# Splitting three weight blocks ahead instead of two, and moving the row flips, in the paired experts of a mixture of 32

## The chip, the cores and the metric

The kernel runs on one core of one Trainium2 chip. The metric is the device time of one execution in microseconds (us); the number that counts is the median of several runs. All engines of the core take part: TensorE (PE), VectorE (DVE), ScalarE (ACT), GpSimd (POOL) and SyncE (SP), whose queue issues the weight transfers.

## The reference, cut to what matters

Two transformer blocks work on 512 rows of 1024 numbers in float32. The second one holds a mixture of 32 experts, four of which are chosen for each row. Only the time of this mixture is touched by the change:

```python
def moe(x, w_router, b_router, w_up, b_up, w_down, b_down):
    ...
    top_v, top_i = lax.top_k(logits, TOP_K)
    w = jax.nn.softmax(top_v, axis=-1)
    flat_e = top_i.reshape(-1)
    order = jnp.argsort(flat_e)
    sorted_e = flat_e[order]
    tok = order // TOP_K
    sizes = jnp.bincount(flat_e, length=N_EXPERTS).astype(jnp.int32)
    xs = xf[tok]
    h = lax.ragged_dot(xs, w_up, sizes) + b_up[sorted_e]
    g, lin = jnp.split(h, 2, axis=-1)
    g = jnp.minimum(g, SWIGLU_LIMIT)
    lin = jnp.clip(lin, -SWIGLU_LIMIT, SWIGLU_LIMIT)
    act = g * jax.nn.sigmoid(SWIGLU_ALPHA * g) * (lin + 1.0)
    y = lax.ragged_dot(act, w_down, sizes) + b_down[sorted_e]
    y = y * w.reshape(-1)[order][:, None].astype(y.dtype)
    return jax.ops.segment_sum(y, tok, num_segments=n).reshape(B, T, D)
```

Here D is 1024 and so is the hidden width, so an expert has 1024x2048 numbers of `w_up` and 1024x1024 of `w_down`, 12.6 MB in all.

## The kernel before, in words

**Blocks and buffers.** The experts are put in an order by their number of rows. The weights of one expert are 12 blocks of 128x2048 float32 (1 MiB each), eight of `w_up2` and four of `w_dn2`, in the sequence of the table `ORDER`. Block n of the whole stream lies in raw buffer n % 8 (`raws`), and `refill(n)` puts the fetch of block n+8, into the buffer that block n leaves, on SP's queue (L1122). The eight buffers carry four names in the listings below: `b_12206` for blocks 0, 1, 8, 9 of a large expert, `pp` for 2, 3, 10, 11, `b_12225` for 4, 5 and `b_12343` for 6, 7.

**A large expert** (`expert`, up to 128 rows) computes with split weights: ACT copies a block into a rounded high part (L219), DVE subtracts it from the block for the low part (L220), and both go into one of four pairs of tiles (block n into pair n % 4). The pairs are called `wh`/`wl` (two of them), `raw` and `b_12224` here. `part` then runs 12 matmuls a block (L1322). After up blocks 3, 5 and 7 the gated product (`gated`, L1345 to L1349) is made on ACT and DVE, and after blocks 5, 8 and 9 it is transposed on PE (`flip`, L1303) and split, as the down blocks' left side `h`. Down blocks 8 and 9 need its first half, 10 and 11 the second.

**A small expert** (`few`, up to 64 rows) multiplies the raw block as it lies (`halves`, L1517 and L1521), without a split.

**The order of the run.** Here the large expert 0 comes first, then eleven pairs of a small expert and a large one (`pairs`), and nine small ones at the end. In the first four pairs the large expert has a second pass (`two`, `SECOND = 4`) with 32 more rows, which multiplies the raw blocks, so that their buffers are refilled only behind that pass.

**Work ahead.** In a paired small expert, blocks 0 and 1 of the large one are split after the small one's blocks 10 and 11 (`unfold`) and not yet refilled. In the large expert, iteration i splits block i+2, refills that buffer, and for i = 0, 1 refills the buffer of block i too. `ahead` also issues the gather of the rows of the expert after the next (POOL, L1289, at i = 2) and transposes the next expert's rows at i = 8 and 9 of a small expert (`flip`, L1303), each half being split by ACT and DVE (0.5 MB of rows for a large expert). The instructions are written in program order; a scheduler then sets each engine's own order, and that is what the listings in the section on the change show.

Below, Lk is block k of the large expert of a pair, and a pair is counted from its small expert's first matmul.

Of the kernel before, what the change touches and what calls it, by code (L numbers as in the profile page):

```python
# [25 lines left out]
NE, TT = 32, 128  # L26
# [131 lines left out]
class K:  # L158
# [941 lines left out]


    ORDER = [("w_up2", c, i) for c in range(8) for i in (c,)] + [("w_dn2", 0, 0), ("w_dn2", 1, 2), ("w_dn2", 0, 1), ("w_dn2", 1, 3)]
    RAW, PAIRS = 8, 4
    TAIL = 0, 1, 4, 3, 2

    def moe_weights(self):
# [17 lines left out]
    def raw(self, n):  # L1124
        return self.raws[n % self.RAW if n < NE * 12 else self.TAIL[n - NE * 12]]

    def unfold(self, n):
        wh, wl = self.pairs[n % self.PAIRS]
        self.split(wh, wl, self.raw(n))
        if n % 12 > 1 or n >= NE * 12:  # L1130
            self.refill(n)

    def refill(self, n):
# [8 lines left out]
    def moe(self):  # L1142
        tc, nc, a = self.tc, self.nc, self.a
        with ExitStack() as es:
            mp = es.enter_context(tc.tile_pool(name="mp", bufs=1))
            m = self.m
            m["mm"] = [self.pm(n, 512) for n in ("mm", "mm", "lg", "lg")]
            m["bb"] = [self.pm("pv", 512) for i in range(2)]
            m["tr"] = [self.pm("tr", 4, 128) for i in range(2)]
            self.ntr = 0  # L1150
            w = lambda n: self.wp.tile([128, 2048], F32R, name=n)
            b2 = self.big.tile([128, 2, 2048], F32R, name="b2")
            b3 = self.big.tile([128, 2, 2048], F32, name="b3")
            self.raws += [b3[:, i] for i in range(2)]
            self.pairs = [(w("wh"), w("wl")), (w("wh"), w("wl")), (w("raw"), w("raw")),
                          tuple(b2[:, i] for i in range(2))]
            b4 = self.big.tile([128, 4, KC, 128], F32R, name="b4")
            m["x"] = [(b4[:, 0], b4[:, 1]), (b4[:, 2], b4[:, 3])]
            self.b4 = b4
            h = mp.tile([128, 2, KC, 128], F32R, name="h")  # L1160
            m["h"] = h[:, 0], h[:, 1]
            xb = self.xb
            m["xb"] = xb[:, 0], xb[:, 1]
            b5 = self.big.tile([128, 4, D], F32, name="b5")
            m["xg"] = [mp.tile([128, D], F32, name="xg"), b5[:, 0]]
            for i, n in enumerate(("y", "act", "actb")):
                m[n] = [b5[:, 1 + i]]
            m["sg"] = mp.tile([128, 512], F32, name="sg")
            m["one"] = [mp.tile([128, 2, 128], F32R, name=f"one{i}") for i in range(2)]
            m["oh"] = [mp.tile([128, TB, 128], BF, name=f"oh{i}") for i in range(2)]  # L1170
            m["xs"] = mp.tile([128, KC, 32], F32, name="xs")
            m["xf"] = mp.tile([128, KC, 64], F32, name="xf")
            m["seven"] = mp.tile([128, 2], F32, name="seven")
            for i, v in enumerate((7.0, float(np.float32(1.702) * np.float32(7.0)))):
                nc.vector.memset(m["seven"][:, i:i + 1], v)
            self.noh = 0
            m["sl"] = [self.slot_tiles(mp, f"s{i}") for i in range(4)]
            self.identb = mp.tile([128, 128], BF, name="identb")
            nc.vector.tensor_copy(self.identb, self.ident)
            m["jb"] = mp.tile([128, 1], F32, name="jb")  # L1180
            m["pos"] = mp.tile([128, TB, 1], F32, name="farpos")
            srt = self.const(mp, "sort")
            m["far"] = mp.tile([128, 2], F32, name="far")
            m["frw"] = mp.tile([128, TB, 1, 6], BF, name="frw")
            m["fw"] = mp.tile([128, TB, 1], F32, name="fw")
            self.slots(m["sl"][0], self.posm[:, :, 0:1], self.rw[:, :, 0:1], only=3)
            nc.vector.memset(m["xg"][1], 0.0)
            first = self.gather(m["xg"][0], m["sl"][0], 0)
            with tc.issue_after(first.ins):
                for n in range(4, 6):  # L1190
                    self.fetch(n, nc.gpsimd)
            self.order(srt)
            b0 = self.big.tile([128, 2, 2048], F32, name="b0")
            self.raws += [b0[:, i] for i in range(2)]
            for n in range(6, self.RAW):
                self.fetch(n)
            for n in range(2):
                self.unfold(n)
            self.select(0)
            self.flip(m["xg"][0], m["x"][0], whole=m["xf"])  # L1200
            self.places(srt)
            for i in (2, 3):
                self.unfold(NE * 12 + i)
            self.embed(self.big.tile([128, TB, D], F32, name="b0"))
        self.rts.close()
# [145 lines left out]
    def bank(self, e, i):  # L1351

        mm, s = self.m["mm"], 2 * (e % 2)
        if i < 8:
            return mm[(s + i // 2) % 4]
        return mm[(s + i % 2) % 4]
# [59 lines left out]
    def expert(self, e, two=False):  # L1416

        nc, m = self.nc, self.m
        one, x, act = m["one"][e % 2], m["x"][e % 2], m["act"][0]
        bank = partial(self.bank, e)  # L1420
        self.numbers(e)
        if two:
            self.second_rows()
        for i in range(12):
            n = e * 12 + i
            if i < 10:
                self.split(*self.pairs[(n + 2) % self.PAIRS], self.raw(n + 2))
                if not two:
                    self.refill(n + 2)
            if i < 2 and not two:  # L1430
                self.refill(n)
            self.part(bank(i), x if i < 8 else m["h"], i, self.pairs[n % self.PAIRS], one)
            if two:
                for k in range(i + (i > 0), min(i + 2, 12)):
                    self.second(k, e)
                    self.refill(e * 12 + k)
            if i == 0 and e:
                self.finish(e - 1, False)
            self.ahead(e, i, 6, False)
            self.swiglu(i, bank, act)  # L1440
            if i in (5, 8, 9):
                self.flip(act, m["h"], *{5: (0, 4), 8: (4, 6), 9: (6, 8)}[i])
        if two:
            self.second_finish()
        self.finish(e, True)
# [77 lines left out]
    def few(self, e, paired=False, second=False):  # L1523

        nc, m = self.nc, self.m
        self.numbers(e)
        xf, act = m["xf"], m["act"][0][:, :512]
        hf = m["y"][0][:, :512].rearrange("p (t a r) -> p t a r", t=4, a=2)
        h = lambda k: hf[:, k % 2, k // 2] if k < 4 else hf[:, k % 2 + 2, k // 2 - 2]
        for i in range(12):  # L1530
            n = e * 12 + i
            self.halves(self.bank(e, i), (lambda k: xf[:, k]) if i < 8 else h, i, e)
            self.refill(n)
            if i > 9 and (paired or e == NE - 1):
                self.unfold(n + 2)
            if i == 0 and e and e % 2 == 0:
                self.finish(e - 1, False)
            self.ahead(e, i, 8, paired)
            if i == 3 and second:
                self.further(e + 1)  # L1540
            if i in (3, 5, 7):
                j = i // 2
                pg, pl = [self.bank(e, k)[:, :256] for k in (0, 2)] if j == 1 else \
                    [self.bank(e, i)[:, 128 * k:128 * k + 128] for k in range(2)]
                self.gated(pg, pl, self.side(act, j, 64))
            if i in (5, 8, 9):
                t0, t1 = {5: (0, 2), 8: (2, 3), 9: (3, 4)}[i]
                p = self.tr()
                for t in range(t0, t1):
                    nc.tensor.transpose(p[:, t - t0], act[:, 128 * t:128 * t + 128], self.ident)  # L1550
                nc.vector.tensor_copy(hf[:, t0:t1].rearrange("p t a r -> p t (a r)"), p[:, :t1 - t0])
            if e == NE - 1 and i == 6:
                self.last_rows(e)
        if e % 2 == 0:
            self.finish(e, False)
        if e == NE - 1:
            self.last(e)

    def ahead(self, e, i, at, both):

        m = self.m
        if i == 1 and e == 0 or i == 6 and e % 4 == 1 and e + 3 < NE:
            f = e // 4 * 4 + 4 if e else 0
            self.slots(m["sl"][f // 4 % 2], self.posx[:, :, f:f + 4], self.rw[:, :, f:f + 4])
        for f in [e + 2] * (i == 2) + [1] * (i == 1 and e == 0):
            if f < NE:
                self.gather(m["xg"][f % 2], m["sl"][f // 4 % 2], f % 4, 64 if f % 2 or at == 8 and e else 128)
        if i == 2 and e + 1 < NE:
            self.select(e + 1)
        if i in (at, at + 1) and e + 1 < NE:  # L1570
            f, k = (e + 1) % 2, 4 * (i - at)
# [367 lines left out]
```

## Time and profile before

| what | us |
|---|---|
| median of 3 runs | 2599.8 (2597.35 to 2602.37) |
| the profiled execution | 2600.15 |
| its span in the trace | 2598.1 |
| mixture: from large expert 0 to the last small one | 1339.4 to 2511.4 |
| four pairs with a second pass | 1385.4 to 1721.2 (82.0, 83.5, 86.4 and 83.9) |
| seven plain pairs | 1721.2 to 2214.8 (72.8, 70.1, 70.8, 68.4, 70.6, 68.4 and 72.6) |
| nine small experts | 2226.9 to 2511.4 |

The profiled execution is 0.35 us above the median, and 2.05 us of it lie outside the span. PE is busy for 93% of the span; its mean granted clock is 0.972 of full speed. A pair's bounds are read from the first matmul of each small expert (L1517) in TensorE's timeline.

### The profile page before, as it was taken

The page shows a single profiled execution, that of the slowest core. Times are in us where ns is not written, and L with a number is a line of the kernel's source. Part 1 is how long each engine was busy: PE and PEld are TensorE (multiplying, and loading weights), DVE is VectorE, ACT ScalarE, POOL GpSimd, SP SyncE. Part 2 cuts the span into 40 slices and gives each one's busy share as a digit, 9 for nine tenths or more (in the row PEclk, how much of TensorE's full clock was granted, in tenths as well). Part 3 has the DMA queues.
Part 4 walks back from the last instruction along what each step waited for, and adds up shares of the span by engine and source line. Part 5 has one row for each costly group of instructions (what it writes and reads, how often), then busy time and mean ns, then how long its engine had stood idle before and what let it go on. Part 6 is the DMA issues. An engine that isn't in the chain of part 4 may idle for free. (4 is left out here: it accounts for less than half of the span.)

```text
span 2598.1 us, 41846 instructions
## 1 busy us (share of the span) xinstructions
PE 2425.4 (93%) x17042; PEld 1941.2 (75%) x17042; DVE 1326.2 (51%) x2473; ACT 1043.5 (40%) x1578; POOL 174.5 (7%) x184
## 2 busy tenths in 40 slices
PE   7999999999999999999989999999999999788888
PEld 5789987898898898898976676666666666554557
DVE  6767753344333344557585466445656666121135
ACT  5755552223223324557353344334444444111133
POOL 0021100000000000000010010110001000000000
PEclk9999999999999999999979999999999999899999
DMA  4122222322222222220378889989999999799990
GB/s 160 65 90 78 74 70 89 127 86 88 98 93 86 98 70 83 75 71 17 109 271 324 305 317 333 341 301 367 381 378 392 385 403 373 294 399 400 407 376 33
DMA packets 86474, 552.63 MB, mean 213 GB/s; under 512 B 11799, under 2 KB 12951, under 8 KB 24936
## 3 DMA queue, kind: packets, MB, share of 16 engines
q1 hardware_dynamic: 71280, 508.33, 50.6%
q0 software_dynamic: 8352, 29.76, 4.7%
q10 hardware_dynamic: 6616, 11.53, 1.3%
q8 instruction: 142, 2.33, 0.4%
q14 instruction: 84, 0.69, 0.1%
HBM read 530.03 MB, written 19.55 MB: 212 GB/s over the span
## 5 line engine op out<-in xcount | busy, mean ns | idle before, releaser
L245 PE MATMUL mm<-b,wh 128*128 128x512 f32 (+1 forms) x1840 | 512.8, 365 | 1.7 <-ACT b L222 0.8
L245 PEld LDWEIGHTS mm<-b,wh 128*128 128x128 f32 x1840 | 328.8, 190 | 65.4 <-issue 3.4
L245 PE MATMUL mm<-b,wl 128*128 128x512 f32 (+2 forms) x920 | 335.2, 365 | 1.3 <-DVE wl L205 1.3
L245 PE MATMUL mm<-wh,b 128*128 128x256 f32 x1488 | 284.3, 287 | 1.5 <-DVE b L675 0.8
L205 DVE TENSOR_TENSOR wl<-raw,wh 128x2048 fp32r<-128x2048 f32 x81 | 185.5, 2290 | 176.2 <-ACT wh L204 176.2
L204 ACT ACTIVATE wh<-raw 128x2048 fp32r<-128x2048 f32 x81 | 155.1, 1915 | 261.2 <-PE mm L245 248.8
L245 PEld LDWEIGHTS mm<-wh,b 128*128 128x128 f32 x1488 | 235.9, 191 | 4.6 <-DVE b L675 1.2
L245 PE MATMUL mm<-wl,b 128*128 128x256 f32 x744 | 213.0, 286 | 1.0 <-DVE wl L205 1.0
L220 DVE TENSOR_TENSOR wl<-b,wh 128x2048 fp32r<-128x2048 f32 x74 | 169.2, 2288 | 65.4 <-ACT wh L219 62.4
L245 PEld LDWEIGHTS mm<-b,wl 128*128 128x128 f32 (+1 forms) x920 | 174.6, 190 | 31.8 <-DVE wl L205 2.2
L1521 PE MATMUL lg<-b,xf 128*64 128x256 f32 x1280 | 154.3, 389 | 14.7 <-DMA b<-w_up 10.1
L219 ACT ACTIVATE wh<-b 128x2048 fp32r<-128x2048 f32 x74 | 141.0, 1908 | 61.8 <-DMA b<-w_up 30.8
L245 PEld LDWEIGHTS mm<-wl,b 128*128 128x128 f32 x744 | 141.9, 191 | 2.5 <-DVE wl L205 1.3
L1521 PEld LDWEIGHTS lg<-b,xf 128*64 128x64 f32 x1280 | 94.3, 139 | 65.7 <-DMA b<-w_up 15.9
L1521 PE MATMUL lg<-b,b 128*64 128x256 f32 x1024 | 130.7, 394 | 7.5 <-DMA b<-w_dn 7.2
L213 POOL TENSOR_TENSOR rs<-rm,c_nhalf 128x1 f32<-128x1 f32 (+3 forms) x52 | 53.0, 1021 | 1158.9 <-DVE rm L211 1150.6
L1521 PEld LDWEIGHTS lg<-b,b 128*64 128x64 f32 x1024 | 76.0, 141 | 49.1 <-issue 11.5
L1345 ACT ACTIVATE sg<-mm,seven 128x128 f32<-128x128 f32 (+2 forms) x48 | 21.8, 455 | 223.2 <-PE mm L1521 180.9
L1521 PE MATMUL mm<-pp,xf 128*64 128x256 f32 x640 | 84.3, 388 | 4.6 <-DMA pp<-w_up 4.5
L1347 DVE SCALAR_TENSOR_TENSOR sg<-lg,sg 128x256 f32<-128x256 f32 (+1 forms) x48 | 19.2, 399 | 127.6 <-ACT sg L1346 127.6
L1521 PE MATMUL mm<-b,xf 128*64 128x256 f32 x640 | 74.8, 383 | 7.0 <-DMA b<-w_up 7.0
L1345 ACT ACTIVATE sg<-lg,seven 128x256 f32<-128x256 f32 (+1 forms) x48 | 21.7, 452 | 146.1 <-PE lg L1521 118.4
(534 smaller groups left out, 4597.9 us busy)
## 6 DMA issues: line engine op xcount, KB each, us to landing
b<-w_up SPq DMA_DIRECT2D x190, 1024.0 KB, 6.7
b<-w_dn SPq DMA_DIRECT2D x96, 1024.0 KB
pp<-w_up SPq DMA_DIRECT2D x64, 1024.0 KB, 13.4
raw<-w_in SPq DMA_DIRECT2D x39, 1024.0 KB, 4.9
pp<-w_dn SPq DMA_DIRECT2D x32, 1024.0 KB, 14.2
raw<-w_up SPq DMA_DIRECT2D x16, 1024.0 KB, 5.8
raw<-w_down SPq DMA_DIRECT2D x16, 1024.0 KB, 4.8
raw<-w_out SPq DMA_DIRECT2D x8, 1024.0 KB, 4.8
```

Of the source, the lines that this page charges most:

```text
L204: nc.scalar.activation(wh, raw, AF.Copy)
L205: nc.vector.tensor_tensor(wl, raw, wh.bitcast(F32), op=OP.subtract)
L213: self.nc.gpsimd.tensor_tensor(r, m, self.c["nhalf"][:, :n], op=OP.pow)
L219: nc.scalar.activation(hi, src, AF.Copy)
L220: nc.vector.tensor_tensor(lo, src, hi.bitcast(F32), op=OP.subtract)
L245: self.nc.tensor.matmul(ps, l, r, start=(i == 0), stop=(i == n - 1))
L1345: nc.scalar.activation(sg, pg, AF.Relu, scale=-1.0, bias=m["seven"][:rows, 0:1])
L1347: nc.vector.scalar_tensor_tensor(sg, pg, 7.0, sg, op0=OP.min, op1=OP.mult)
L1521: nc.tensor.matmul(o[n], x(4 * kh + k), cut(w[:, k], n), start=not up and kh == k == 0, stop=kh == 1 and k == 3)
```

## The change

A constant `LEAD = 3` takes the place of the two blocks of lead. In a paired small expert, three blocks (L0, L1, L2) are split, after its blocks 9, 10 and 11, and outside the pairs with a second pass their raw buffers are refilled at once. In `expert`, iteration i splits block i+3. The transposes of the next large expert's rows stand at the small expert's blocks 4 and 5 instead of 8 and 9. In `moe`, the blocks L0 to L2 of expert 0 are split before the loop.

```diff
-    RAW, PAIRS = 8, 4
+    RAW, PAIRS, LEAD = 8, 4, 3
...
-    def unfold(self, n):
+    def unfold(self, n, keep=False):
         wh, wl = self.pairs[n % self.PAIRS]
         self.split(wh, wl, self.raw(n))
-        if n % 12 > 1 or n >= NE * 12:
+        if not keep:
             self.refill(n)
...
-            for n in range(2):
-                self.unfold(n)
+            for n in range(self.LEAD):
+                self.unfold(n, keep=True)
...
         for i in range(12):
             n = e * 12 + i
-            if i < 10:
-                self.split(*self.pairs[(n + 2) % self.PAIRS], self.raw(n + 2))
-                if not two:
-                    self.refill(n + 2)
-            if i < 2 and not two:
+            if i + self.LEAD < 12:
+                self.unfold(n + self.LEAD, keep=two)
+            if i < self.LEAD and not e:
                 self.refill(n)
             self.part(bank(i), x if i < 8 else m["h"], i, self.pairs[n % self.PAIRS], one)
...
             self.refill(n)
-            if i > 9 and (paired or e == NE - 1):
+            if paired and i + self.LEAD > 11:
+                self.unfold(n + self.LEAD, keep=second)
+            if e == NE - 1 and i > 9:
                 self.unfold(n + 2)
...
-            self.ahead(e, i, 8, paired)
+            self.ahead(e, i, 4 if paired else 8, paired)
...
-                self.gather(m["xg"][f % 2], m["sl"][f // 4 % 2], f % 4, 64 if f % 2 or at == 8 and e else 128)
+                self.gather(m["xg"][f % 2], m["sl"][f // 4 % 2], f % 4, 64 if f % 2 or at != 6 and e else 128)
```

The last line keeps its meaning. Three places of the engines' orders follow, all of the plain pair with large expert 12.

DVE, the end of the pair, before. `b_12206` as source is L8 or L9, `pp` L10 or L11; L1347 to L1349 are the gated product that needs L7; `h` is the left side of L10 and L11; `xf` holds the next small expert's rows.

```order
L220 TENSOR_TENSOR raw<-pp,raw 128x2048
L1307 COPY xf<-tr 128x256
L220 TENSOR_TENSOR wl<-b_12206,wh 128x2048
L1347 SCALAR_TENSOR_TENSOR sg<-lg,sg 128x256
L1348 TENSOR_SCALAR b_12234<-lg 128x4x64
L1349 SCALAR_TENSOR_TENSOR b_12234<-b_12234,sg 128x4x64
L220 TENSOR_TENSOR b_12224<-pp,b_12224 128x2048
L220 TENSOR_TENSOR wl<-b_12206,wh 128x2048
L220 TENSOR_TENSOR h<-tr,h 128x256 x2
```

The same place with the change (`b_12343` is L7):

```order
L220 TENSOR_TENSOR wl<-b_12206,wh 128x2048
L1349 SCALAR_TENSOR_TENSOR b_12234<-b_12234,sg 128x4x64
L1307 COPY xf<-tr 128x256 x2
L220 TENSOR_TENSOR b_12224<-b_12343,b_12224 128x2048
L220 TENSOR_TENSOR raw<-pp,raw 128x2048
L220 TENSOR_TENSOR b_12224<-pp,b_12224 128x2048
L1347 SCALAR_TENSOR_TENSOR sg<-lg,sg 128x256
L1348 TENSOR_SCALAR b_12234<-lg 128x4x64
L1349 SCALAR_TENSOR_TENSOR b_12234<-b_12234,sg 128x4x64
L220 TENSOR_TENSOR h<-tr,h 128x256 x2
```

The gated product stood ahead of the split of L11; now it stands behind it, and the split of L9 comes ahead of that of L7.

PE, from the transposes (L1303) on which `h` for L10 and L11 rests, before; behind these rows follow the rest of L9's twelve matmuls, ten of L10 (`raw`) and twelve of L11 (`b_12224`).

```order
L1303 MATMUL tr<-c_ident,b_12234 128x128 x4
L1322 MATMUL mm<-wh,h 128x512
L1322 MATMUL mm<-raw,h 128x512 x2
L1322 MATMUL mm<-wl,h 128x512
L1322 MATMUL mm<-wh,h 128x512 x2
L1322 MATMUL mm<-wl,h 128x512
```

The same place with the change, to the pair's end:

```order
L1322 MATMUL mm<-wl,h 128x512
L1322 MATMUL mm<-wh,h 128x512
L1322 MATMUL lg<-b_12224,b_12232 128x512 x11
L1303 MATMUL tr<-c_ident,b_12234 128x128 x4
L1322 MATMUL mm<-raw,h 128x512 x12
L1322 MATMUL mm<-b_12224,h 128x512 x12
```

L9's matmuls used to come after the transposes; now the eleven of L7 (`lg<-b_12224`) come last before them, and only L10 and L11 follow.

SP's queue, the fetches for the large expert's second half, before (`ISA` is a wait or an address; the load reads the next expert's number):

```order
L1122 DMA b_12343<-w_up 128x2048
L1122 ISA
L1122 DMA b_12343<-w_up 128x2048
L1379 TENSOR_LOAD ovi
L1122 ISA
L1122 DMA pp<-w_dn 128x2048
L1122 ISA
L1122 DMA b_12206<-w_dn 128x2048
L1122 ISA
L1122 DMA pp<-w_dn 128x2048
L1122 ISA
L1122 DMA b_12206<-w_dn 128x2048
```

The same fetches with the change:

```order
L1122 DMA b_12206<-w_dn 128x2048
L1122 ISA
L1122 DMA b_12343<-w_up 128x2048
L1122 ISA
L1122 DMA b_12206<-w_dn 128x2048
L1122 ISA
L1122 DMA b_12343<-w_up 128x2048
L1122 ISA
L1122 DMA pp<-w_dn 128x2048
L1379 TENSOR_LOAD ovi
L1122 ISA
L1122 DMA pp<-w_dn 128x2048
```

L6 and L7 now stand behind L8 and L9, one after each. In the four pairs with a second pass SP's order is the same as before.

## Rows read from the trace of the kernel before

**Rows 1.** The page, span in 40 slices, busy share of the DMA engines in tenths.
```profile
DMA  4122222322222222220378889989999999799990
```
**Rows 2.** Windows of three stretches: four second-pass pairs, seven plain pairs, nine small experts.
```profile
core 0: us, PE busy (x) PEld busy (x) DVE busy (x) ACT busy (x) POOL busy (x), PEclk, DMA share, GB/s
1385.37:1721.21 335.84, 325.17 (x3290) 228.47 (x3290) 188.94 (x339) 144.04 (x172) 31.14 (x24) 0.97 0.87 321
1721.21:2214.80 493.59, 460.45 (x2753) 321.67 (x2752) 287.66 (x391) 226.99 (x231) 42.60 (x29) 0.97 0.98 380
2226.90:2511.40 284.50, 244.56 (x1996) 152.46 (x1996) 55.07 (x174) 32.21 (x73) 18.01 (x15) 0.97 0.99 392
```
**Rows 3.** Waits of PE, plain pairs: us in total, times, longest us.
```profile
PE mm L1322 <- DVE wl L220: 28.4, 16, 2.4
```
**Rows 4.** Waits of PE, the four pairs with a second pass.
```profile
PE tr L1459 <- DVE b L220: 7.7, 2, 4.1
PE mm L1322 <- DVE wl L220: 1.7, 2, 0.8
```
**Rows 5.** Timeline of PE, end of large expert 12: start, us, instruction, [idle before <-releaser].
```profile
1844.85 2.81 PE L1322 MATMUL lg<-b,b 128*128 128x512 f32 x11
...
1853.30 0.60 PE L1303 MATMUL tr<-c_ident,b 128*128 128x128 f32 x4
...
1854.16 0.73 PE L1322 MATMUL mm<-raw,h 128*128 128x512 f32 x2
1856.16 0.50 PE L1322 MATMUL mm<-wl,h 128*128 128x512 f32 x1 [1.27 <-DVE wl L220]
...
1861.17 2.96 PE L1322 MATMUL mm<-b,h 128*128 128x512 f32 x12
1864.06 0.65 PE L1517 MATMUL lg<-bup,one 128*64 128x256 f32 x4
```
**Rows 6.** Timeline of DVE, large expert 12.
```profile
1821.29 0.68 DVE L220 TENSOR_TENSOR b<-tr,b 128x512 fp32r<-128x512 f32 x1
...
1845.75 2.29 DVE L220 TENSOR_TENSOR raw<-pp,raw 128x2048 fp32r<-128x2048 f32 x1 [0.80 <-ACT raw L219]
...
1850.49 0.42 DVE L1347 SCALAR_TENSOR_TENSOR sg<-lg,sg 128x256 f32<-128x256 f32 x1
...
1851.62 2.28 DVE L220 TENSOR_TENSOR b<-pp,b 128x2048 fp32r<-128x2048 f32 x1
1853.82 2.28 DVE L220 TENSOR_TENSOR wl<-b,wh 128x2048 fp32r<-128x2048 f32 x1
```
**Rows 7.** Timeline of ACT, end of large expert 12.
```profile
1847.70 0.48 ACT L1345 ACTIVATE sg<-lg,seven 128x256 f32<-128x256 f32 x1 [0.17 <-PE lg L1322]
...
1848.62 1.89 ACT L219 ACTIVATE b<-pp 128x2048 fp32r<-128x2048 f32 x1
```
**Rows 8.** Timelines of DVE and PE, end of large expert 14.
```profile
1924.60 2.28 DVE L220 TENSOR_TENSOR wl<-b,wh 128x2048 fp32r<-128x2048 f32 x1
...
1934.82 0.65 PE L1517 MATMUL lg<-bup,one 128*64 128x256 f32 x4
```
**Rows 9.** Timeline of POOL, the gather that the small expert ahead of large expert 12 issues.
```profile
1815.44 0.99 POOL L1289 DMA_INDIRECT xg<-xs,s1i  x1 [17.52 <-PE tr L1550]
```
**Rows 10.** Windows: a stretch in large expert 12; the start of the small expert behind it.
```profile
1821.80:1825.10 3.30, 3.30 (x9) 2.63 (x8) 3.27 (x5) 2.36 (x3) 0.00 (x0) 0.50 1.03 426
1865.40:1867.40 2.00, 2.00 (x22) 1.35 (x20) 0.00 (x0) 0.00 (x0) 1.70 (x2) 1.00 0.66 70
```
**Rows 11.** Timelines of DVE and PE, start of large expert 4, a pair with a second pass.
```profile
1493.78 2.29 DVE L220 TENSOR_TENSOR wl<-b,wh 128x2048 fp32r<-128x2048 f32 x1 [4.42 <-ACT wh L219]
...
1496.73 0.68 PE L1459 MATMUL tr<-c_ident,b 32*128 32x32 f32 x8 [4.08 <-DVE b L220]
...
1498.26 0.63 PE L1322 MATMUL mm<-wl,b 128*128 128x512 f32 x1
```
**Rows 12.** Timeline of ACT, the high part of L0 in large expert 12.
```profile
1817.14 1.91 ACT L219 ACTIVATE wh<-b 128x2048 fp32r<-128x2048 f32 x1 [3.91 <-DMA b<-w_up]
```

## Prediction

> **What bounds the kernel now.** The page's slices come first: the reader sees the share of the DMA engines climb to nine tenths in the last third, where the mixture runs [rows 1]. The windows then split the mixture into its stages. In the four pairs with a second pass PE is busy for 325.17 of 335.84 us at a DMA share of 0.87, so there the matmuls bind. In the seven plain pairs PE is busy for 460.45 of 493.59 us at a DMA share of 0.98 and 380 GB/s, and the small experts alone draw 392 [rows 2]: PE and DMA are both near their end, and 33 us of PE's idle time are left to win. The waits name it: 28.4 us, 16 times, on the low part that DVE makes (L220) [rows 3]; in the pairs with a second pass it is 7.7 and 1.7 us [rows 4]. The end of large expert 12, engine by engine, stands for all seven plain pairs. PE waits there 1.27 us for L9's low part, the last split on DVE [rows 5], and DVE runs from split to split [rows 6].
>
> So a plain pair ends like this: DVE's last split ends at 1853.82 + 2.28 = 1856.10, and what PE has left, L9's and the rest of L10's and L11's matmuls, lasts until 1864.06 [rows 5, 6]. While DVE splits L9, PE has other things to do: the gated product and the transposes for L10 and L11 are finished before.
>
> **The change, part by part.**
>
> *Removed ahead of the last split that an up or early down block needs.* With the change DVE's list puts four things behind the splits of L0 to L9, or out of the large expert's start, that stood ahead of one of them before: the splits of L10 (2.29) and L11 (2.28), the last gated product (from 1850.49 to the next start at 1851.62, 1.13) and the second half of the rows' split (0.68), all from [rows 6]. That is 6.38 us, and the last of those splits, now L7's, would end at 1856.10 - 6.38 = 1849.72. PE needs 0.06 to start, as it did behind L9's (1856.16 against 1856.10) and 2.81 for L7's eleven matmuls [rows 5]: L7 is done at 1852.59.
>
> *Added behind it.* Now a chain follows that nothing covers, since L8 and L9 are already multiplied. ACT waits 0.17 for PE and makes the first step of the gated product, 0.48; then comes L11's high part, 1.89 [rows 7], whose pair of tiles L7's matmuls have to leave first; DVE makes the low part, 2.28, and only then its share of the gated product, 1.13 [rows 6]; transposes and the split of `h` take 1854.16 - 1853.30 = 0.86 [rows 5]. Together 6.81: L10 starts at 1859.40. L10 and L11 are 24 matmuls, twice the 1864.06 - 1861.17 = 2.89 that L11 took [rows 5], so 5.78, and the pair ends at 1865.18 against 1864.06: **1.12 later**. Large expert 14 ends its last split at 1924.60 + 2.28 = 1926.88 and itself at 1934.82 [rows 8]; the same steps give 1935.96, 1.14 later. For seven pairs 7 x 1.13 = **+7.9**. The fetches support it rather than help: L6 and L7 now stand behind L8 and L9 on SP's queue, whose issue waits until DVE has split L0 and L1, so L7 lands later than before.
>
> The bounds: where L6's or L7's data come later still, all of that is added; where the DVE queue gets 2.29 further ahead, it is 1.13 - 2.29 = -1.16 a pair. A plain pair thus lies between -1.2 and, with the 2.4 us of the longest wait on a low part [rows 3] on top, +3.5. I take the sum, as it is read row by row.
>
> *Moved: the flips and the gather.* In the pair of large expert 12 the gather was held on POOL until PE's transposes had freed its target, 17.52 us [rows 9]. The flips end some blocks earlier, so its 128 rows of 4 KB, 0.52 MB, now travel ahead of L0's block. At the 426 GB/s of the busy stretch [rows 10] this takes 1.23 us, and L0's high part already waits for its data, 3.91 us [rows 12]. In every second plain pair, three in all, that is **+3.7**. If the transfers find room elsewhere it is 0. In the others the gather waits for its slots, not for the flip: 0. The eight transposes themselves lie beside PE's other matmuls before and after, 0.60 per four [rows 5]; their cover is DMA time in the small expert, and without it they would cost the same either way.
>
> *Pairs with a second pass.* There `keep` leaves the refills and SP's order where they were, so it is only the splits that move. In large expert 4 the split of L0 ends at 1493.78 + 2.29 = 1496.07, the second half of the rows followed, the second pass' transposes waited 4.08 behind it, and L0's first matmul on the low part came at 1498.26 [rows 11]. With the flips gone from there it can start at 1496.13, 2.13 earlier; the gather ahead of L0 takes 1.23 back, so -0.9. This form occurs twice, -1.8; the other two wait on L0's data alone, 0. Together **-1.8**. The bounds are all start waits gone, -9.4 [rows 4], and four times the 1.13 of a gated product that comes late, +4.5.
>
> *Expert 0.* The split of L2, 2.29 on DVE, moves into the routing ahead; it lies in front of the loop instead of in it, so **0**, between -2.3 and +2.3. The fetches are issued in nearly the same order.
>
> **Sum.** 7.9 + 3.7 - 1.8 + 0 = +9.8 on the profiled execution's 2600.15, so **2610**. This execution is 0.35 above the median, which makes no difference here. What a measurement of this kernel can tell from no change is about 0.2%, 5.2 us.
>
> **The rivals.**
>
> *The clock goes down too.* Each pair's new tail has PE idle for about 6 us. In large expert 12, behind a start wait, the granted clock is 0.50 for 3.30 us, the lower of its two levels [rows 10]; that costs half, 1.65. Once more per plain pair makes 7 x 1.65 = 11.6, so 2621.5. For it: the low clock follows PE's waits in this trace. Against it: the start wait and its dip may go away, and the small expert's beginning is short of data anyway. The Trainium skill, in "TensorE: Matmul & The Clock Gate" under "Why this matters for your kernels", warns of idle gaps between bursts of matmuls, since the throughput then drops; by it this rival would be the likeliest one. The trace agrees that a drop follows a gap, but not behind every one.
>
> *DMA sets the pair's length, and nothing changes.* The share of 0.98 speaks for it [rows 2]. Against it speaks the pause at each small expert's start, 0.66 and 70 GB/s in [rows 10], where all buffers are full and wait for PE. Then it is 2600.
>
> *Faster: the third split of lead holds.* If ACT and DVE do L2's split inside the small expert, DVE is one split, 2.29, ahead through the whole large expert. Then the plain pairs give 7 x (1.13 - 2.29) = -8.1, the pairs with a second pass 4 x -2.29 = -9.2, and the gather takes +3.7: 2586.5. It decides by whether the data of L2 are in before the small expert ends. Against it: L0's high part already waited 3.91 us for its block [rows 12], and L2 is fetched two blocks behind L0, so a further split in advance finds nothing to split. For it: refilling at once brings the down blocks earlier. The Trainium skill, in "DMA: Bandwidth & Descriptors" under "Rules for kernel authors", wants a DMA issued early and waited for late, which is what this change does for L8 to L10; by that rule alone the time would fall. The rows do not bear it out where the queue issues them ahead of blocks that are needed sooner.
>
> **How the numbers follow.** The forecast has 0.49, the low clock on top 0.11, DMA as the bound 0.21, faster 0.19. The first two make slower by over 0.2% 0.60; within 0.2% is 0.21; faster by over 0.2% is 0.19. The range begins at 2590, where the faster case has half of its gain in the second-pass pairs and the rest in full (-8.1 - 4.6 + 3.7 = -9.0, 2591), and leaves out that case in full; it ends at 2625, the low clock with three of the 4.5 us that are the second-pass pairs' upper bound. The likeliest sign's own range is 2605 to 2625.
>
> **What would show it.** Right: SP issues L8 ahead of L6 and L9 ahead of L7 in the plain pairs; DVE's list runs from split to split until L7 some 6 us earlier than before; PE stands 5 to 7 us before the four transposes ahead of L10, released by the gated product (L1349); plain pairs of 69 to 74 us, 1 to 2 longer than before; waits on L8's and L9's low parts gone. Wrong: L2 split before the small expert's last matmul and PE's wait at the large expert's start gone; the last gated product found ahead of L11's split; plain pairs of 69 us or less; or a DMA share that stays at 0.98 with pairs of the same length.

## The result and the profile after

The changed kernel takes 2627.86 us (median of 4 runs, 2619.65 to 2631.96) against 2598.57 for the kernel before measured with it: a ratio of 1.0111 (95% interval 1.0088 to 1.0135), so slower by 29 us. All ratios below are to the kernel before, measured alongside, with that interval. The forecast was 2610, slower; the sign came out, the size did not, and the time lies above the range, which ended at 2625.

The profiled execution takes 2625.09, 24.9 more than the one before. By stages, read from the first matmul of each small expert: the mixture starts 4.6 earlier (the code ahead of it hardly differs; the traces of this study put this start anywhere from 1334 to 1340), expert 0 takes 1.9 more, the four pairs with a second pass 4.3 less, the seven plain pairs 33.5 more (73.0 to 77.3 us each), and the last nine experts 1.7 less. The windows of the same three stages as in [rows 2]:

```profile
1382.75:1714.29 331.54, 323.61 (x3288) 226.63 (x3289) 187.67 (x337) 143.16 (x172) 34.59 (x24) 0.98 0.88 325
1714.29:2240.00 525.71, 470.37 (x2753) 326.98 (x2752) 288.06 (x391) 225.27 (x232) 54.57 (x29) 0.95 0.92 358
2253.50:2536.20 282.70, 244.19 (x1996) 152.56 (x1996) 54.98 (x174) 32.18 (x73) 17.98 (x15) 0.97 1.00 394
```

In the middle row PE and DMA both stand idle more than before: PE's idle time grew from 33 to 55 us, the DMA share fell from 0.98 to 0.92, and the granted clock from 0.97 to 0.95. The waits of PE in the plain pairs have another head than [rows 3]:

```profile
PE tr L1303 <- DVE b L1349: 34.2, 7, 5.8
PE mm L1322 <- DVE wl L220: 10.3, 6, 1.8
PE lg L1322 <- DVE raw L220: 4.6, 4, 1.1
```

The 28.4 us on low parts have become 10.3, and the four transposes ahead of L10 now wait for the last gated product, once in each of the seven pairs, 34.2 us in all (5.8 us in three pairs, 4.2 in four). The end of large expert 12 on PE answers to [rows 5] (in the changed file L1517 is L1515):

```profile
1848.00 2.69 PE L1322 MATMUL lg<-b,b 128*128 128x512 f32 x11
1856.51 1.11 PE L1303 MATMUL tr<-c_ident,b 128*128 128x128 f32 x4 [5.82 <-DVE b L1349]
1857.67 4.20 PE L1322 MATMUL mm<-raw,h 128*128 128x512 f32 x12
1861.70 2.94 PE L1322 MATMUL mm<-b,h 128*128 128x512 f32 x12
1864.57 0.65 PE L1515 MATMUL lg<-bup,one 128*64 128x256 f32 x4
```

L7's eleven matmuls end at 1850.69, and nothing is left for PE until the transposes. So it is in three of the plain pairs. In the other four, large experts 10, 14, 18 and 22, seven of L9's matmuls still stand behind L7's, and PE's wait is that much shorter. Large expert 14:

```profile
1922.77 2.70 PE L1322 MATMUL lg<-b,b 128*128 128x512 f32 x11
1925.31 0.63 PE L1322 MATMUL mm<-wh,h 128*128 128x512 f32 x2
...
1926.71 0.40 PE L1322 MATMUL mm<-wh,h 128*128 128x512 f32 x1
1931.29 0.66 PE L1303 MATMUL tr<-c_ident,b 128*128 128x128 f32 x4 [4.19 <-DVE b L1349]
```

Below, "the gap" is the whole time from the last up matmul to L10, 6.7 to 7.0 us in every pair; PE stands idle for 4.2 to 5.8 us of it. ACT and DVE at the end of large expert 12, answering to [rows 7] and [rows 6]:

```profile
1850.73 0.47 ACT L1345 ACTIVATE sg<-lg,seven 128x256 f32<-128x256 f32 x1 [3.86 <-PE lg L1322]
1851.10 1.90 ACT L219 ACTIVATE b<-pp 128x2048 fp32r<-128x2048 f32 x1
1852.90 0.50 ACT L1346 ACTIVATE sg<-sg,seven 128x256 f32<-128x256 f32 x1
```

```profile
1853.03 2.29 DVE L220 TENSOR_TENSOR b<-pp,b 128x2048 fp32r<-128x2048 f32 x1 [3.09 <-ACT b L219]
1855.24 0.42 DVE L1347 SCALAR_TENSOR_TENSOR sg<-lg,sg 128x256 f32<-128x256 f32 x1
...
1856.03 0.43 DVE L1349 SCALAR_TENSOR_TENSOR b<-b,sg 128x256 f32<-128x256 f32 x1
```

This is the forecast chain, instruction for instruction: the gated product's first step, L11's split on ACT and on DVE, and only then the rest of the gated product. From the end of L7 to the start of L10 it takes 1857.67 - 1850.69 = 6.98; the forecast had 6.81. But L10's twelve matmuls then take 4.20 where L11's take 2.94. Windows over the 24 matmuls of L10 and L11 show why, for the first three plain pairs of the change:

```profile
1783.58:1791.67 8.09, 8.09 (x26) 6.16 (x28) 1.03 (x3) 1.06 (x2) 0.00 (x0) 0.69 0.43 178
1857.67:1864.64 6.97, 6.97 (x26) 5.38 (x28) 2.33 (x11) 1.06 (x2) 0.00 (x0) 0.82 0.70 288
1932.21:1939.45 7.24, 7.24 (x26) 5.57 (x28) 0.93 (x3) 0.91 (x2) 0.00 (x0) 0.79 0.53 216
```

and for two pairs of the kernel before:

```profile
1858.37:1864.13 5.76, 5.76 (x27) 4.39 (x27) 0.00 (x0) 0.69 (x1) 0.00 (x0) 1.00 1.01 424
1929.13:1934.89 5.76, 5.76 (x27) 4.38 (x27) 0.00 (x0) 0.69 (x1) 0.00 (x0) 1.00 1.01 421
```

The granted clock is 0.69 to 0.82 on average where it was 1.00: part of the stretch runs at the lower level, 1.2 GHz, behind the gap. The other four plain pairs read 0.68, 0.79, 0.68 and 0.77. (The kernel before lost clock elsewhere: PE's wait for L8's low part, 2.2 to 2.4 us in every plain pair, was followed by matmuls at 1.2 GHz in five of the seven.)

So the seven plain pairs, measured from the small expert's first matmul to the large one's last, grew by 31.8 us together, and the forecast's steps can be set against the trace one by one (each sum is over the seven, with the last split of each pair of the kernel before taken as for large experts 12 and 14):

| step | forecast | measured | difference |
|---|---|---|---|
| pair against before, by the chain alone | +7.5 | +31.8 | +24.3 |
| of it: the last up matmul is done later | 0 | +10.9 | +10.9 |
| of it: from there to L10 | 7 x 6.81 = 47.7 | 48.1 | +0.4 |
| of it: L10's and L11's matmuls | 7 x 5.78 = 40.5 | 53.4 | +12.9 |

(With each pair's own rows the first line is +7.5; the prediction, from two of them, had +7.9. The gather's +3.7 stood in the forecast besides and is part of the 10.9.)

What makes the last up matmul late shows on ACT, first at L8's high part. Large expert 14 with the change:

```profile
1903.68 1.91 ACT L219 ACTIVATE wh<-b 128x2048 fp32r<-128x2048 f32 x1
1909.30 1.92 ACT L219 ACTIVATE wh<-b 128x2048 fp32r<-128x2048 f32 x1 [3.71 <-PE lg L1322]
1911.12 1.90 ACT L219 ACTIVATE raw<-b 128x2048 fp32r<-128x2048 f32 x1
```

The row in the middle is L8, whose pair of tiles L4's matmuls have to leave, 3.71 us of waiting; the row behind it is L6, which needs the pair that L2's matmuls leave, and those come before L4's. L8 stands ahead of L6 because it was fetched ahead of it. DVE waits in turn, 43.3 us on the high parts in `wh` in the plain pairs where it was 30.4, and PE waits up to 1.1 us for L6's low part (the 4.6 us on `raw` above).

ACT's waits in the plain pairs, two with the change and one before, show a second cause, the data of the first blocks:

```profile
ACT wh L219 <- DMA b<-w_up: 31.3, 13, 5.9
ACT wh L219 <- PE lg L1322: 26.2, 7, 3.8
```

```profile
ACT wh L219 <- DMA b<-w_up: 16.7, 6, 3.9
```

The 26.2 us are L8's wait, once a pair. It is also there with the flips back (24.7 us), and absent before, with the flips alone and with the fetches in the order of use: it goes with the order of the fetches. The wait for data is 31.9 us with the flips alone and 16.4 with the flips back: it goes with the flips and the earlier gather. In return ACT waits less for the data of later blocks, 1.6 us where it was 9.5.

### The profile page after: what moved, and what is told of

The parts are those of the page before. It is cut to its first block, busy times and chain, and to the rows that moved or that the text cites. A ratio compares the mean times of both kernels' runs of the same rounds, so it can differ in the third digit from the quotient of the medians.

```text
span 2623.0 us, 41900 instructions
## 1 busy us (share of the span) xinstructions
PE 2430.8 (93%) x17042; PEld 1942.6 (74%) x17042; DVE 1324.8 (51%) x2473; ACT 1040.3 (40%) x1578; POOL 189.7 (7%) x184
## 5 line engine op out<-in xcount | busy, mean ns | idle before, releaser
L1519 PE MATMUL lg<-b,xf 128*64 128x256 f32 x1280 | 154.2, 389 | 12.9 <-DMA b<-w_up 9.7
L1347 DVE SCALAR_TENSOR_TENSOR sg<-lg,sg 128x256 f32<-128x256 f32 (+1 forms) x48 | 19.2, 399 | 128.0 <-ACT sg L1346 127.9
L1519 PE MATMUL mm<-b,xf 128*64 128x256 f32 x640 | 77.3, 385 | 6.7 <-DMA b<-w_up 6.7
```

Of the source, the lines that this page charges most:

```text
L1347: nc.vector.scalar_tensor_tensor(sg, pg, 7.0, sg, op0=OP.min, op1=OP.mult)
L1519: nc.tensor.matmul(o[n], x(4 * kh + k), cut(w[:, k], n), start=not up and kh == k == 0, stop=kh == 1 and k == 3)
```

## The experiments

Four questions: is it the order of fetches and splits, or the third block of lead, or the moved flips; is the longer stretch of L10 and L11 the clock's; how much of the gap is L11's split; and which version beats both kernels.

**Fetches in the order of use, three blocks of lead.** The refills of L0 to L2 are issued behind the small expert's last block:

```diff
-                self.unfold(n + self.LEAD, keep=second)
+                self.unfold(n + self.LEAD, keep=True)
...
+        if e and not two:
+            for i in range(self.LEAD):
+                self.refill(e * 12 + i)
         for i in range(12):
```

> The change, but the buffers of L0 to L2 of a plain pair are refilled after the small expert's last block, so that SP fetches L4 to L11 in the order of use. Theory (the order of the fetches, and with it that of the splits, makes the loss): L8 and L9 are split and multiplied behind L7 again and cover the gated product, so PE's gap of 7 us ahead of L10 goes (7 x 7 = 49 less at most, the lower clock behind it included), the plain pairs come to 67 to 70 us and the kernel to 2580 to 2600. Rival (the third block of lead or the moved flips cost by themselves): the plain pairs stay at 73 to 76 us and the kernel at 2615 to 2630.

Measured: 2581.08, ratio to before 0.9931 (0.9915 to 0.9948). Not only does the loss go, it beats the kernel before. The plain pairs come to 66.5 to 69.6 us and the gap's wait has left the list; PE's waits there are

```profile
PE mm L1322 <- DVE wl L220: 11.7, 7, 1.8
PE mm L1322 <- DVE b L220: 4.6, 7, 1.1
```

The third block of lead and the moved flips are both still in this kernel, so neither of them makes the loss by itself. One thing stays unexplained: the pairs with a second pass take 335.9 us here, as before the change, though their flips are moved.

**Flips back at blocks 8 and 9,** all else of the change kept:

```diff
-            self.ahead(e, i, 4 if paired else 8, paired)
+            self.ahead(e, i, 8, paired)
```

> The change, but the row flips stand at the small expert's blocks 8 and 9, as before. Theory (fetch order): L8 and L9 are still fetched ahead of L6 and L7, the plain pairs keep their gap of 7 us ahead of L10 and 73 to 76 us; the pairs with a second pass lose the 4 us that they gained; 2615 to 2635. Rival (the flips and the earlier gather cost): plain pairs of 69 to 71 us, 2595 to 2605.

Measured: 2619.49, ratio 1.0078 (1.0061 to 1.0095). Still slower than before, with a gap of 6.7 to 7.0 us ahead of L10 in every plain pair, and 24 matmuls in 6.7 to 7.4 us behind it. The plain pairs take 71.9 to 75.6 us, the first one 80.6. The pairs with a second pass take 336.8 us, as before, instead of 331.5. How much of the 10.9 us by which the last up matmul was late belongs to the flips can't be read from it: in six of the plain pairs that lateness falls from 10.0 to 5.0 us, but in the first one it grows from 1.0 to 5.5, in a profiled execution (2629.38) that is 10 above this kernel's median.

**The flips alone,** on the kernel before (the other line of `ahead` as in the change):

```diff
-            self.ahead(e, i, 8, paired)
+            self.ahead(e, i, 4 if paired else 8, paired)
```

> The kernel before with the flips moved to blocks 4 and 5, two blocks of lead and the late refills. Theory: the second-pass pairs gain 1 to 4 us together, the plain pairs change by -0.7 (the half of the rows is out of the way of L0's and L1's splits) to +1.2 us each (the gather travels ahead of L0): 2592 to 2605. Rival (the flips cost by themselves): 2615 or more.

Measured: 2600.09, ratio 1.0004 (0.9991 to 1.0017): no difference. The profile shows two terms that cancel, at about the size of the forecast: the second-pass pairs take 332.0 instead of 335.8 us, the plain pairs 508.8 instead of 505.7. Each is read from one profiled execution.

**Refilled at once with two blocks of lead,** flips in their old place:

```diff
-        if n % 12 > 1 or n >= NE * 12:
+        if not keep:
             self.refill(n)
...
-            if i < 2 and not two:
+            if i < 2 and not e:
                 self.refill(n)
```

(`keep` is set where the change sets it.)

> The kernel before, with two blocks of lead and the flips in their old place, but L0's and L1's buffers refilled at once in plain pairs. SP fetches L8 between L6 and L7, and L9 behind L7. Theory: L9's twelve matmuls still stand between L7 and the transposes for L10, which cover 2.9 to 5 us of the gated product's chain, so the gap ahead of L10 is 2 to 4 us instead of 7 and the kernel comes to 2595 to 2612. Rival (refilling at once costs as such, by the wait on SP's queue): 2615 to 2630.

Measured: 2586.18, ratio 0.9950 (0.9933 to 0.9968), faster than expected. L8 is fetched between L6 and L7 here, L9 behind both. The gap between the last up matmul and L10 is 3.7 to 3.8 us, filled by L9's matmuls. The pairs split into two kinds: 65.0 us in three, 71.8 in three (the first takes 69.6). So refilling at once does not cost by itself. This kernel and the one with the flips back differ by the lead alone: with refills at once, the third block costs 33 us. What it changes in the queue is that L9 too then comes ahead of L7; in the order of use (below) the third block costs nothing that can be told.

**Idle matmuls in the gap.** Fourteen matmuls whose result nobody reads there, all else as in the change:

```diff
+            if i == 8 and e and not two:
+                for k in range(14):
+                    nc.tensor.matmul(m["bb"][0], x[0][:, 0], self.pairs[3][0][:, :512], start=True, stop=True)
```

> The change, with 14 idle matmuls (128x512) on TensorE in the gap ahead of L10 of each plain pair; they multiply L11's high part, as soon as ACT has made it, into a bank that nobody reads there, and change no other order. Theory (the stretch of L10 and L11 is longer than 5.75 us because the granted clock is at its lower level behind the gap): it falls from 7.0 to 8.3 us to under 6.5, 13 us less over seven pairs at most: 2612 to 2622. Rival (it is longer because h or the split of L11 is late): no gain, 2622 to 2635.

Measured: 2614.45, ratio 1.0059 (1.0040 to 1.0078), 13.4 below the change, and the two intervals don't meet. The windows over L10 and L11 in its first three plain pairs:

```profile
1781.89:1787.74 5.85, 5.85 (x26) 4.49 (x28) 0.93 (x3) 0.91 (x2) 0.00 (x0) 1.00 0.68 283
1854.65:1860.48 5.83, 5.83 (x26) 4.50 (x28) 2.24 (x11) 0.92 (x2) 0.00 (x0) 1.00 0.63 261
1927.79:1933.62 5.83, 5.83 (x26) 4.50 (x28) 0.94 (x3) 0.91 (x2) 0.00 (x0) 1.00 0.65 271
```

The clock is 1.00 in all seven and the stretches sum to 40.9 us instead of 53.4. The work that PE had to do grew, and the kernel became faster: the 12.9 us of the table are the clock's. In the three pairs without L9's matmuls in the gap, PE still waits 2.36 us ahead of the idle matmuls; the clock falls at about the end of that wait and is back at 1.00 ahead of L10. So in large expert 12:

```profile
1849.02:1852.43 3.41, 3.41 (x9) 2.63 (x10) 3.25 (x4) 0.23 (x1) 0.00 (x0) 0.50 1.01 420
```

There the 14 matmuls end after the chain and make the gap 1.0 to 1.1 longer, which takes some of the gain back.

**L11's split behind the gated product.** Ordering edges on ACT and DVE, for plain pairs only:

```diff
-            if i + self.LEAD < 12:
+            if i == 8 and e and not two:
+                with self.tc.issue_after(self.gate[0].ins), self.tc.issue_after(self.gate[1].ins):
+                    self.unfold(n + self.LEAD)
+            elif i + self.LEAD < 12:
                 self.unfold(n + self.LEAD, keep=two)
```

(`gate` holds the instructions of L1346 and L1349.)

> The change, with the split of L11 in plain pairs ordered behind the last gated product on ACT and on DVE. Theory (the split of L11, 1.89 on ACT and 2.28 on DVE, stands in the uncovered chain): the transposes ahead of L10 come some 4 us earlier, but the low part of h then stands behind L11's split on DVE, so that L10 ends only 1 to 2 us earlier; 7 to 14 us in all, or more where the shorter gap keeps the clock up: 2605 to 2622. Rival (the gap is set by the data of L10 and L11, not by the order): no gain, 2622 to 2635.

Measured: 2608.18, ratio 1.0039 (1.0021 to 1.0057), 20 below the change, more than the 7 to 14 that I expected. Gap and matmuls together take 77.9 us in the seven pairs instead of 101.5. The gap falls to 3.3 to 3.5 us; the matmuls of L10 and L11 still take 7.2 to 8.6. In the four pairs with L9's matmuls in the gap, PE stands idle for 0.7 us of it, the clock stays at 1.00, and a wait of 1.0 us for L11's low part makes the 7.2. In the other three, PE stands idle for 2.35 us, the clock behind it averages 0.67 to 0.80, and the matmuls take 8.5 to 8.6. The end of large expert 14, one of the four, on PE:

```profile
1923.64 0.66 PE L1303 MATMUL tr<-c_ident,b 128*128 128x128 f32 x4 [0.72 <-DVE b L1349]
1924.55 0.72 PE L1322 MATMUL mm<-raw,h 128*128 128x512 f32 x2 [0.26 <-ACT h L219]
1925.11 0.40 PE L1322 MATMUL mm<-b,h 128*128 128x512 f32 x1
1926.52 0.50 PE L1322 MATMUL mm<-b,h 128*128 128x512 f32 x1 [1.01 <-DVE b L220]
```

Even so it stays slower than before: part of the chain can be reordered away, but the rest of it, the later last up matmul and, in three pairs, the lower clock stay.

**Fetches in the order of use, two blocks of lead,** on the kernel before:

```diff
+            if i == 0 and e and not two:
+                self.refill(n)
+                self.refill(n + 1)
             if i < 10:
...
-            if i < 2 and not two:
+            if i < 2 and not e:
                 self.refill(n)
```

> The kernel before (two blocks of lead, flips at blocks 8 and 9) with L0's and L1's buffers refilled at the start of the large expert in the order of use, so that SP fetches L8, L9, L10, L11 where it was L10, L8, L11, L9. Theory (the order of the fetches decides): most of the gain of the version in block order comes with two blocks of lead as well: 2578 to 2592. Rival (the third block of lead gives the gain once the order is right): 2593 to 2602.

Measured: 2580.51, ratio 0.9920 (0.9889 to 0.9950). The gain can't be told from that with three blocks of lead. The kernel before was not in the order of use either: it fetched L10, L8, L11, L9, and L9's split came last. Its plain pairs now show

```profile
1723.17:2211.06 487.89, 455.58 (x2753) 317.03 (x2753) 287.87 (x391) 227.29 (x232) 44.19 (x30) 0.97 0.99 387
```

a DMA share of 0.99 at 387 GB/s, against 392 in the small experts alone [rows 2].

**Order of use, three blocks of lead, flips back.** One line differs from the first experiment, the `ahead` line as above.

> The version with three blocks of lead and fetches in block order, with the flips back at blocks 8 and 9. Theory (the flips are worth nothing in plain pairs): 2578 to 2590, plain pairs within 1 us of those with the flips moved. Rival (the early flips make the room for the third split): 2592 or more.

Measured: 2579.00, ratio 0.9920 (0.9889 to 0.9950): the flips make no difference here that can be told. From the kernel with the flips back above, 2619.49, this one differs only in when the buffers of L0 to L2 are refilled, and so in the order of the fetches.

**Order of use, two blocks of lead, flips early in the second-pass pairs,** and **early in all pairs**:

> Two blocks of lead, fetches in the order of use, and the flips at blocks 4 and 5 in the four pairs with a second pass alone. Theory (the parts add up): 2.5 to 4 us below the version with two blocks of lead and fetches in order, 2574 to 2580. Rival (the gain in the second-pass pairs is given back at the pairs behind): 2580 to 2586.

> The same with the flips at blocks 4 and 5 in all pairs; beside the kernel with three blocks of lead in block order it differs by the lead alone. Theory (the lead is worth nothing and the earlier gather costs 0 to 3 us in plain pairs): 2575 to 2583. Rival (three blocks of lead are worth their room): 2584 to 2590.

Measured: 2581.66, ratio 0.9924 (0.9900 to 0.9947), and 2577.76, ratio 0.9910 (0.9887 to 0.9933). The second is the fastest kernel of the study by its ratio, 23 us below the one before, but the intervals of all five versions in the order of use overlap. Whether the second-pass gain of some 4 us adds up could not be told.

## Why the prediction was right or wrong

**Right: the order and the chain.** SP fetches L8 ahead of L6 and L9 ahead of L7; PE stands before the four transposes, released by L1349; the chain behind L7 takes 6.98 in large expert 12 where 6.81 was summed, and 48.1 against 47.7 over the seven pairs. So the sign was no luck. Large expert 12 did not stand for all seven in one thing: in four of them, seven of L9's matmuls are left for the gap, which shortens PE's wait there but not the chain. The idle matmuls and the ordering edges hit exactly this place.

**Wrong, first: "L10 and L11 are 24 matmuls, twice the 1864.06 - 1861.17 = 2.89 that L11 took [rows 5], so 5.78".** That duration comes from a stretch at full clock, and the same step had just put a chain of 6.81 us ahead of it in which PE stands idle. Measured are 7.0 to 8.3, in all 12.9 us more over the seven pairs. The low clock stood among the rivals, priced at 11.6 from one stretch of [rows 10], which is close as a sum; single pairs lost 1.2 to 2.5 where 1.65 was taken. But it had a chance of 0.11, among other grounds because not every gap is followed by a drop; here every one of the seven was. The rule of the Trainium skill in "TensorE: Matmul & The Clock Gate", section "Why this matters for your kernels", warns of idle gaps between bursts of matmuls. The trace agrees with it, the clock averaging 0.68 to 0.82 behind the gaps and 1.00 once they were filled. Even with this rival the sum was 2621.5, some 6 us short of the 2627.86 measured; the second step, below, is not in it.

**Wrong, second: "the last of those splits, now L7's, would end at 1856.10 - 6.38 = 1849.72".** This took DVE to run from split to split in the new order as it did in the old one. It did nearly so in large expert 12 (0.5 late), but over the seven pairs the last up matmul came 10.9 late. The gather's +3.7 is in it, and about that size was measured with the flips alone (+3.1 in the plain pairs), though not where it was put: the wait for the data of the first blocks grew in all seven plain pairs, not in three. (By the kernel's text the gather of [rows 9] is issued by large expert 12 itself, for the 128 rows of large expert 14; the prediction's size is right.) For the other 7 the trace shows ACT waiting at L8 for L4's pair of tiles, with L6 queued behind it, 26.2 us in the seven pairs; that this is all of it was not tried by itself. The prediction looked only at SP for what L8 holds up, and not at the two engines that split.

**Right in its sign, open in its size: the second-pass pairs.** -1.8 was forecast, -4.3 measured, and -3.8 with the flips alone. Of the 4.3 us one pair, that of large expert 6, gives 3.7. The 7.7 us wait of the second pass' transposes [rows 4] is gone from the list of waits, while that on low parts went from 1.7 to 5.2. Other traces shift by as much without the flips' doing: in the order of use with three blocks of lead these pairs take 335.9 us with the flips moved and 333.3 with the flips back.

**The other rivals.** "DMA sets the pair's length" fell: the DMA share went down to 0.92. With the order right the share is 0.99, so that DMA may then set the length; no run tests it. "The third split of lead holds" fell too: with the order right, no difference between two and three blocks of lead can be told, so the lead was worth nothing by itself. The rule of the Trainium skill in "DMA: Bandwidth & Descriptors", section "Rules for kernel authors", to issue early, did not decide: the blocks that were issued early went ahead of ones that were needed sooner.

## What to carry to other kernels

When buffers are refilled as early as they come free, see in which order the fetches then stand on the queue, and whether the engines behind it take the blocks in that order: here a block that was fetched early was split early, and stood ahead of one needed sooner on SP's queue, on ACT and on DVE. Work that a later block brings is also the cover for a chain of small steps; where a change makes that work finish early, price the chain uncovered, and see what it would cost if what follows ran at the lower clock. And look at the order of the fetches in the kernel that you start from: here two refills moved were worth 0.8%.

## What was not expected of the hardware

Adding 98 idle matmuls made the kernel 13 us faster: with fourteen in each of seven gaps the granted clock was 1.00 over the next 24 matmuls, which took 5.8 us instead of 7.0 to 8.3. In three of the gaps it had fallen to 0.50 at about the end of a wait of 2.36 us, and rose again while the idle matmuls ran. All seven gaps of the change, with PE idle for 4.2 to 5.8 us, were followed by a stretch at the lower level; idle stretches of 2.2 to 2.4 us were followed by one in five of seven pairs of the kernel before, and in all three with L11's split behind the gated product.
